# A hybrid attention and state-space layer: rotary turning of all queries, then of all keys, in place of block by block

## The chip, the cores and the metric

The kernel runs on one core of a Trainium2 chip. The metric is the device time of one execution in microseconds (us); lower is better. Every quoted window, such as 392 to 440, is in us from the start of the profiled span.

## The reference

The layer works on 2048 tokens of width 1024, in float32. The normalised input is projected once; the columns of the product are the queries, keys and values of a differential attention (4 heads, two softmax maps each, head size 64, values of 128) and the input of a diagonal state space model (S5). Both results go through one output projection, and a SwiGLU feed-forward layer and a last norm follow. Cut to what matters here:

```
hn = rms_norm(h, norm1_g)
q, k, v, u = split(hn @ w_in, [512, 1024, 1536])
q = partial_rope(q, cos, sin)      # the first 16 of 64 columns are rotated
k = partial_rope(k, cos, sin)
attn = diff_attention(q, k, v, lam)
ssm  = s5_mixer(u, ...)            # ends in y * sigmoid(y @ w_glu + b_glu)
h = h + concat(norm(attn), ssm) @ w_out
h = h + (silu(hn2 @ w_gate) * (hn2 @ w_up)) @ w_down
```

The rotation multiplies a column by a cosine and adds its partner, eight columns away, times a signed sine. The tables of cosines and sines depend on the token alone, so queries and keys share them.

## The kernel before, in words

**Matmuls.** Every product is made of three matmuls: an operand is split into a rounded high part (an ACT cast) and a rest (a DVE or POOL subtraction), and high times high, high times low and low times high are summed in PSUM (`mm3`, L516; `split`, L505). The tokens are cut into NB = 4 blocks of 512.

**Phase 1** (`phase1`, from L629) computes, in the order of the program text: the norm, the projections for the state space model, its preparation, its 16 pairs of groups (`ssm_pair`, L1020), the projections of those 16-column pieces of the queries and keys that are not rotated (L756), the values of two heads (`values(0, mm)`, L784), the rotated pieces ("q", 0) and ("k", 0) (L786 to L813), and the values of the other two heads (`values(1, mm[2:4])`, L815). Phase 2 (`phase2`, L1110) computes the gated unit after the state space model (`glu`, L1440; "the GLU" from here on), the output projections, the attention and the feed-forward layer.

**Who sets the order.** The program text doesn't. Each statement is recorded as a task with an estimated cost, its memory dependencies and a priority (`Rec`, L297; `Sched`, L176). A planner runs through the tasks and emits at each step the one that can start first; among those within 0.05 us of each other it takes the one with the lowest priority number. The engines then execute their own instructions in the order emitted. Rotations and their stores have -75, weight loads with their splits -95, projections -40, the units of the attention 0 and up, and the GLU 1000 and up. An edit in one place can thus reorder work on all engines afterwards.

**One rotation** (L803 to L813) is: 24 matmuls into one of four PSUM banks (`proj`, L669); an ACT copy of the bank into a tile `r`; a permutation matmul of `r` into the PSUM bank `tp2[0]`; on DVE that bank times the sine into `r2`; `r` times the cosine, and the sum of both, on DVE or POOL; the split (cast and subtraction) into a staging tile `z`; the store of `z` to memory, one DMA for a query (`qD`, 512 KB), two for a key (`kD`, 256 KB each: the high part, then the rest). `r` has two tiles (`turned`), `z` has two (`ups`, taken in turn, which the values after it take in turn as well), `r2` and `tp2[0]` are single.

**The tables.** `table(b)` loads the cosine and the sine of a block, two DMAs of 256 KB from `rD`, into one of two pairs of tiles. Tables 0 and 1 are loaded ahead of the loop and tables 2 and 3 in it, when the block two before has been turned. There are eight such DMAs in all.

**The weights.** Split weights lie in three slots (`ws`, L634), taken in turn by the 16 calls of `wload`. The last five calls are ("v", 1), ("q", 0), ("k", 0), ("v", 2), ("v", 3), and ("v", 3) gets the slot of ("q", 0). Raw weights pass through one single tile, the area RAW (`raws`, L635); the split of ("v", 3) is the last that reads it.

**What takes over the memory.** Areas that phase 1 has finished with become buffers of phase 2 (`room`, L1449 in `glu`). Of the three load buffers `yr` of the GLU, one is the area RAW (L1463), one lies in SD with the rotation's tables and `r2` (L1461), one in UP with the staging tiles (L1464). In a `yr` buffer come first the two halves of `w_glu` (L1473), which are cast on ACT (L1479) and subtracted on POOL or DVE (L1480), then the results of the state space model (`yD`, L1486; cast L1493, subtraction L1496). The GLU's matmuls come in groups of 24 into one PSUM tile, `fx`.

Of the kernel before, what the change touches and what calls it, by code (L numbers as in the profile page):

```python
# [14 lines left out]
AF = mybir.ActivationFunctionType  # L15
ALU = mybir.AluOpType
# [9 lines left out]
NB = S // 512  # L26
# [473 lines left out]
class K:  # L500
# [128 lines left out]
    def phase1(self):  # L629
        nc, tc, A, S = self.nc, self.tc, self.A, self.S  # L630
        rec = self.rec = self.nc = Rec(S, nc)
        misc = [a.tile for a in self.misc]
        p = Carve(misc[WS])
        ws = [p.tile([128, 2, 1024], F32R) for _ in range(3)]  # L634
        raws = [misc[RAW]]  # L635
        p = Carve(misc[UP])
        ups = [p.tile([128, 1024], F32R) for _ in range(2)]
        p = Carve(misc[SA], misc[SC])
# [9 lines left out]
        p = Carve(misc[SB])  # L648
# [5 lines left out]
        def turn(kind, tiles):  # L654
            count[kind] += 1
            return tiles[(count[kind] - 1) % len(tiles)]
# [12 lines left out]
        def proj(key, b, banks=mm):  # L669
            w = W[key].rearrange("p z (k c) -> p z k c", k=KD)  # L670
            t = turn("mm", banks)
            for k in range(KD):
                self.mm3(t, w[:, 0, k], w[:, 1, k], hn[b][0][k], hn[b][1][k], k == 0, k == KD - 1)
            return t
# [26 lines left out]
        c = Carve(*(a.tile for a in self.hnb[3]))  # L701
# [35 lines left out]
        p, c = Carve(misc[SA]), Carve(misc[SD])  # L737
# [3 lines left out]
        tables = [c.tile([128, 512]) for _ in range(2)]  # L741
# [10 lines left out]
        def store(key, b, z):  # L752
            (self.qst if key[0] == "q" else self.kst)[b][key[1]] = self.store_qk(key, b, z)

        rec.pri, rec.fair = -40.0, False
        for key in [("q", 1), ("q", 2), ("q", 3), ("k", 1), ("k", 2), ("k", 3)]:  # L756
            wload(key)
            for b in range(NB):
                t = proj(key, b)
                z = turn("up", ups).rearrange("p (c t) -> p c t", c=4)  # L760
# [27 lines left out]
        rot = [self.s2.tile([128, 512], F32, name="rot", tag=n) for n in ("tr", "t1", "t2", "pq")]  # L788
        tables, turned, r2 = [rot[0:2], tables], rot[2:4], self.gy

        def table(b):
            for j in range(2):
                rec.sync.dma_start(out=tables[b % 2][j],
                                   in_=self.rD[j][:, 512 * b:512 * b + 512][None].to_broadcast([8, 16, 512]))

        table(0)
        table(1)
        for b in range(NB):
            cos, sin = tables[b % 2]
            if b in (1, 2):  # L800
                table(b + 1)
            for key, r in zip((("q", 0), ("k", 0)), turned):
                t = proj(key, b)  # L803
                with rec.urgent(-75.0):
                    rec.scalar.activation(out=r, in_=t, func=AF.Copy, scale=0.125 if key[0] == "q" else 1.0)
                    t2 = self.tp2[0]
                    rec.tensor.matmul(t2, lhsT=self.cst["perm"], rhs=r, start=True, stop=True)
                    rec.vector.tensor_tensor(out=r2, in0=t2, in1=sin, op=ALU.mult)
                    rec.any.tensor_tensor(out=r, in0=r, in1=cos, op=ALU.mult)
                    rec.any.tensor_tensor(out=r, in0=r, in1=r2, op=ALU.add)  # L810
                    z = turn("up", ups).rearrange("p (c t) -> p c t", c=4)
                    self.split_qk(key, z, r)
                    store(key, b, z)  # L813

        values(1, mm[2:4])  # L815
        self.hn_end = [S.join(*rec.users(*(a.tile for a in self.hnb[b]))) for b in range(NB)]
# [1377 lines left out]
```

## Time and profile before

| | us |
|---|---|
| median of three executions | 2430.85 |
| lowest and highest | 2430.6, 2438.7 |
| the profiled execution's own time | 2428.99 |
| its span in the trace | 2426.9 |
| granted TensorE clock, mean over the span | 0.985 |

The profiled execution lies 1.86 us below the median, and 2.09 us of it lie outside the span. VectorE (DVE) is busy for 67% of the span, ScalarE (ACT) and GpSimd (POOL) for 43% each. In the views, PE is TensorE's matmuls, PEld its weight loads, SPq the queue from which SyncE issues nearly all DMAs. A bracket at the end of a row gives how long the engine was idle before it and what ended that. L364 is the helper through which all of phase 1 is emitted, so there the tiles tell what a row is: `pair<-hn,misc` is a projection, `pair<-misc,hn` the values, `tp<-misc,cst` the permutation matmul, and L518 to L520 with `fx` are GLU matmuls.

### The profile page before, as it was taken

The numbers are of one execution on the slowest core, as the hardware profiler recorded it, in microseconds if no ns is written. First come the engines' busy times: TensorE is split into PE (matmuls) and PEld (weight loads), VectorE is DVE, ScalarE is ACT, GpSimd is POOL, SyncE is SP. The second block draws the span as 40 slices with busy tenths as digits, with TensorE's granted clock in tenths as the row PEclk, the third lists the DMA queues.
The fourth block names the chain that finished last, engine by engine and source line by source line (L and its number), as shares of the span: only waits on it lengthen the run. The fifth ranks groups of instructions, "written<-read, shape, count | busy, mean of one in ns | idle before, by whom it ended". The sixth has DMA issues, their size and how long they took to land.

```text
span 2426.9 us, 34139 instructions
## 1 busy us (share of the span) xinstructions
PE 2335.0 (96%) x11832; PEld 1958.1 (81%) x11832; DVE 1616.7 (67%) x2577; ACT 1048.9 (43%) x2103; POOL 1041.0 (43%) x1048
## 2 busy tenths in 40 slices
PE   7999999989999999998999999999999999999998
PEld 6887797878888888876788888788888878878876
DVE  7885775247887778647877455754544576585698
ACT  7222333247877776545332333533333342242343
POOL 4134675355666556546544322222232223232244
PEclk9999999999999999998999999999999999999999
DMA  6467675665566557787886232532223255575664
GB/s 216 132 191 215 225 220 170 208 215 156 191 199 193 191 187 245 232 294 234 270 285 223 74 97 81 187 109 78 87 72 96 84 165 198 171 256 165 201 201 162
DMA packets 312174, 435.34 MB, mean 179 GB/s; under 512 B 42241, under 2 KB 187713, under 8 KB 312001
## 3 DMA queue, kind: packets, MB, share of 16 engines
q1 hardware_dynamic: 309408, 428.71, 55.4%
q10 hardware_dynamic: 2592, 4.45, 0.5%
q8 instruction: 93, 1.52, 0.3%
q14 instruction: 81, 0.66, 0.1%
HBM read 287.66 MB, written 145.42 MB: 178 GB/s over the span
## 4 chain that ended last, share of the span: by engine, by line
PE 70%; DMA 6%; DVE 4%; issue 3%; POOL 2%; ACT 2%; SPq 0%; POOLq 0%; DVEq 0%; ACTq 0%
PE pair L519 9%; PE pair L520 9%; PE pair L518 9%; PE tp L519 4%; PE tp L520 4%; PE tp L518 4%; PE fx L518 4%; PE fx L519 3%; PE fx L520 3%; PE pv L518 3%; PE pv L519 3%; PE pv L520 3%; PE pair L364 3%; DMA hn<-qD 2%; PE tp L1320 2%
## 5 line engine op out<-in xcount | busy, mean ns | idle before, releaser
L1782 ACT CAST misc<-hn 128x512 fp32r<-128x512 f32 (+1 forms) x340 | 204.8, 609 | 484.2 <-POOL hn L1902 163.0
L519 PE MATMUL pair<-hn,misc 128*128 128x512 f32 x925 | 363.4, 393 | 10.0 <-DVE hn L1783 9.9
L518 PE MATMUL pair<-hn,misc 128*128 128x512 f32 x925 | 362.2, 392 | 0.5 <-ACT misc L1782 0.4
L520 PE MATMUL pair<-hn,misc 128*128 128x512 f32 x925 | 361.9, 391 | 0.2 <-DVE misc L1783 0.2
L1783 DVE TENSOR_TENSOR misc<-hn,misc 128x512 fp32r<-128x512 f32 (+1 forms) x340 | 247.8, 732 | 113.7 <-ACT misc L1782 113.3
L364 PE MATMUL pair<-hn,misc 128*128 128x512 f32 x1152 | 282.8, 399 | 0.0
L364 PEld LDWEIGHTS pair<-hn,misc 128*128 128x128 f32 x1152 | 215.3, 191 | 45.7 <-issue 2.4
L1902 POOL TENSOR_TENSOR hn<-misc,hn 128x512 f32<-128x512 f32 (+1 forms) x68 | 99.9, 1469 | 296.5 <-DVE misc L1783 296.0
L519 PEld LDWEIGHTS pair<-hn,misc 128*128 128x128 f32 x925 | 174.6, 189 | 51.1 <-DVE hn L1783 15.6
L1909 POOL TENSOR_TENSOR hn<-hn 128x512 f32<-128x512 f32 (+1 forms) x68 | 97.1, 1428 | 256.7 <-DVE misc L1783 240.3
L518 PEld LDWEIGHTS pair<-hn,misc 128*128 128x128 f32 x925 | 174.4, 189 | 38.5 <-ACT misc L1782 0.8
L520 PEld LDWEIGHTS pair<-hn,misc 128*128 128x128 f32 x925 | 174.8, 189 | 36.5 <-DVE misc L1783 0.6
L1899 POOL TENSOR_TENSOR misc<-hn 128x512 f32<-128x512 f32 (+1 forms) x68 | 92.9, 1366 | 245.8 <-DVE misc L1783 200.1
L1221 DVE TENSOR_REDUCE small<-pair 128x1 f32<-128x1024 f32 (+7 forms) x160 | 158.2, 992 | 57.3 <-PE pair L1203 27.0
L1237 ACT ACTIVATE hn<-pair,small 128x1024 f32<-128x1024 f32 (+4 forms) x192 | 166.2, 868 | 60.1 <-DVE small L1221 27.1
L519 PE MATMUL tp<-hn,misc 128*128 128x512 f32 x454 | 177.6, 391 | 3.9 <-DVE hn L1783 3.9
L518 PE MATMUL tp<-hn,misc 128*128 128x512 f32 x454 | 177.4, 391 | 2.1 <-ACT misc L1782 1.9
L520 PE MATMUL tp<-hn,misc 128*128 128x512 f32 x454 | 177.2, 390 | 0.0
L364 POOL TENSOR_TENSOR misc<-misc,misc 128x512 f32<-128x512 f32 (+1 forms) x71 | 84.4, 1190 | 162.8 <-DVE misc L364 130.2
L1946 DVE TENSOR_TENSOR misc<-pair,misc 128x512 f32<-128x512 f32 x110 | 75.9, 690 | 95.9 <-PE pair L520 95.6
L364 POOL TENSOR_TENSOR misc<-misc 128x256 f32<-128x256 f32 (+1 forms) x128 | 102.2, 809 | 44.3 <-DVE misc L364 20.0
L364 DVE TENSOR_TENSOR misc<-misc,misc 128x512 f32<-128x512 f32 (+7 forms) x111 | 93.9, 864 | 36.5 <-ACT misc L364 30.5
(268 smaller groups left out, 5724.5 us busy)
## 6 DMA issues: line engine op xcount, KB each, us to landing
hn<-vD SPq DMA_DIRECT2D x48, 512.0 KB
hn<-kD SPq DMA_DIRECT2D x96, 256.0 KB
hn<-in_w_gate SPq DMA_DIRECT2D x44, 512.0 KB
hn<-in_w_up SPq DMA_DIRECT2D x44, 512.0 KB
fD<-misc SPq DMA_DIRECT2D x88, 256.0 KB
misc<-in_w_down SPq DMA_DIRECT2D x77, 256.0 KB
hn<-qD SPq DMA_DIRECT2D x128, 128.0 KB
hD<-misc SPq DMA_DIRECT2D x32, 512.0 KB
```

The source lines that it names most:

```text
L364: getattr(ENGINE[t.at](self.real), f)(*map(now, args), **{n: now(x) for n, x in kw.items()})
L518: nc.tensor.matmul(out, lhsT=ah, rhs=bh, start=start, stop=False, **k)
L519: nc.tensor.matmul(out, lhsT=ah, rhs=bl, start=False, stop=False, **k)
L520: nc.tensor.matmul(out, lhsT=al, rhs=bh, start=False, stop=stop, **k)
L1221: v.tensor_reduce(out=nl[:, i:i + 1], in_=x.got[sc][:, 0:w], axis=AX.X, op=ALU.max, negate=True)
L1237: a_.activation(out=z.got[rings[i]][:, 0:w], in_=x.got[sc][:, 512 * i:512 * i + w], func=AF.Exp, bias=st(n, n + 1), accum_out=acc)
L1782: hf = lambda t: a_.copy(out=dst(t)[0], in_=src())
L1783: lf = lambda t: (g_ if t.at == "pool" else v).tensor_sub(out=dst(t)[1], in0=src(), in1=dst(t)[0].bitcast(F32))
L1899: s1 = any_(n, lambda t, e: e.tensor_tensor(out=t.got[s1r][:, 0:n], in0=q(1, 0), in1=q(1, 1), op=ALU.add), *r, take=[s1r], pri=pri())
L1902: s2 = any_(n, lambda t, e: e.tensor_sub(out=q(0, 0), in0=s1.got[s1r][:, 0:n], in1=q(0, 0)), s1, s3, a11, pri=pri())
L1909: s4 = any_(n, lambda t, e: e.tensor_sub(out=q(0, 1), in0=q(0, 1), in1=q(0, 0)), s2, a12, pri=pri())
L1946: return S("dve", 1.042e-3 * w + 0.07, lambda t: v.tensor_tensor(out=(t if to is None else to).got[tm], in0=x.got[bank], in1=y.got[tm], op ...
```

## The change

The loop over blocks with queries and keys inside becomes one loop over eight rotations, first the four blocks of the queries, then the four of the keys. Both weights are still loaded ahead of the loop, and the work of one rotation is unchanged. The tile `r` still alternates. The pair of table tiles now alternates with every rotation and not with every block, and each rotation has a load of its own: table(i + 1) is recorded at rotation i (for i from 1 to 6) and may overwrite the tiles of rotation i - 1. Sixteen table DMAs take the place of eight.

```diff
-        def table(b):
+        def table(i):
+            b = i % NB
             for j in range(2):
-                rec.sync.dma_start(out=tables[b % 2][j],
+                rec.sync.dma_start(out=tables[i % 2][j],
                                    in_=self.rD[j][:, 512 * b:512 * b + 512][None].to_broadcast([8, 16, 512]))
 
         table(0)
         table(1)
-        for b in range(NB):
-            cos, sin = tables[b % 2]
-            if b in (1, 2):
-                table(b + 1)
-            for key, r in zip((("q", 0), ("k", 0)), turned):
-                t = proj(key, b)
-                with rec.urgent(-75.0):
...
+        for i in range(2 * NB):
+            key, b, r = (("q", "k")[i // NB], 0), i % NB, turned[i % 2]
+            cos, sin = tables[i % 2]
+            if 0 < i < 2 * NB - 1:
+                table(i + 1)
+            t = proj(key, b)
+            with rec.urgent(-75.0):
...
```

The left-out lines are those of one rotation, the same before and after but for their indentation.

More of the change, by code (lines that the diff above doesn't have):

```diff
@@ L797, in phase1 @@
         table(1)
-        for b in range(NB):
-            cos, sin = tables[b % 2]
-            if b in (1, 2):
-                table(b + 1)
-            for key, r in zip((("q", 0), ("k", 0)), turned):
-                t = proj(key, b)
-                with rec.urgent(-75.0):
[L805 to L813, printed above, removed]
+        for i in range(2 * NB):
[5 more added lines that the diff above has]
+            with rec.urgent(-75.0):
+                rec.scalar.activation(out=r, in_=t, func=AF.Copy, scale=0.125 if key[0] == "q" else 1.0)
+                t2 = self.tp2[0]
+                rec.tensor.matmul(t2, lhsT=self.cst["perm"], rhs=r, start=True, stop=True)
+                rec.vector.tensor_tensor(out=r2, in0=t2, in1=sin, op=ALU.mult)
+                rec.any.tensor_tensor(out=r, in0=r, in1=cos, op=ALU.mult)
+                rec.any.tensor_tensor(out=r, in0=r, in1=r2, op=ALU.add)
+                z = turn("up", ups).rearrange("p (c t) -> p c t", c=4)
+                self.split_qk(key, z, r)
+                store(key, b, z)
         values(1, mm[2:4])
```

## The prediction, made before the change was run

> **What bounds the kernel now.** I read first the page's busy times, then the granted clock and busy share by window, then the time lines of the engines around the rotations, and last the chain of waits.
>
> ```profile
> span 2426.9 us, 34139 instructions
> PE 2335.0 (96%) x11832; PEld 1958.1 (81%) x11832; DVE 1616.7 (67%) x2577; ACT 1048.9 (43%) x2103; POOL 1041.0 (43%) x1048
> ```
>
> TensorE is busy for 2335.0 of 2426.9 us. The change removes no matmul, so it can win only from the 91.9 us in which PE is idle, and from a lowered clock. The windows say where that is:
>
> ```profile
> core 0: us, PE busy (x) PEld busy (x) DVE busy (x) ACT busy (x) POOL busy (x), PEclk, DMA share, GB/s
> 392.00:440.00 48.00, 47.98 (x230) 37.58 (x229) 18.84 (x27) 14.21 (x26) 25.95 (x19) 1.00 0.45 143
> 444.00:446.00 2.00, 2.00 (x11) 2.00 (x11) 0.00 (x0) 1.05 (x2) 0.35 (x1) 0.50 0.90 239
> 454.00:456.00 2.00, 2.00 (x11) 2.00 (x11) 0.00 (x0) 0.00 (x0) 0.00 (x0) 0.50 0.93 316
> 440.00:460.00 20.00, 14.86 (x98) 14.66 (x99) 2.48 (x5) 4.53 (x10) 8.02 (x7) 0.83 0.89 264
> ```
>
> From 392 to 440, where the eight rotations lie, PE is never idle (47.98 of 48): nothing is to be won there, whatever the order. In the next 20 us it is idle for 5.14, and the clock falls to 0.50 in two windows. The time line of PE shows both stalls:
>
> ```profile
> 443.36 7.32 PE L364 MATMUL pair<-misc,hn 128*128 128x256 f32 x48 [3.38 <-DVE misc L364]
> 452.46 7.52 PE L364 MATMUL pair<-misc,hn 128*128 128x256 f32 x48 [1.77 <-DVE misc L364]
> 459.81 0.28 PE L518 MATMUL fx<-misc,misc 128*128 128x256 f32 x1
> 462.69 6.01 PE L364 MATMUL pair<-misc,hn 128*128 128x256 f32 x48
> ```
>
> These are the values after the rotations. Tiles 0 and 1 run inside the rotations' last us; tiles 2 and 3 start after 3.38 us of idling, tiles 4 and 5 after 1.77. The same 48 matmuls take 7.32 and 7.52 us behind the stalls and 6.01 later on, so the lowered clock costs 1.31 and 1.51. Together the stretch loses 3.38 + 1.77 + 1.31 + 1.51 = 7.97 us. After the first four value tiles comes one GLU group of 24 matmuls, from 459.81 to 462.69, 2.88 us.
>
> By the Trainium skill (TensorE: Matmul & The Clock Gate, Part 1) TensorE falls to half clock only after an idle window of about 3.4 us. The trace agrees for the stall of 3.38 and not for that of 1.77, behind which 454 to 456 still shows 0.50. By the rule a stall of 3.0 us, which my sum keeps below, would cost no clock and the gain would be 1.3 us more; the measurement decides.
>
> **Why PE stalls there.** The time line of ACT:
>
> ```profile
> 430.29 1.05 ACT L364 CAST misc<-misc 128x1024 fp32r<-128x1024 f32 x1 [2.48 <-PE pair L364]
> 439.21 1.14 ACT L1479 CAST misc<-misc 128x512 fp32r<-128x512 f32 x2 [2.00 <-DMA misc<-in_w_glu]
> 442.48 0.37 ACT L364 CAST misc<-pair 128x256 fp32r<-128x256 f32 x1 [1.61 <-DMA qD<-misc]
> 444.95 1.14 ACT L1479 CAST misc<-misc 128x512 fp32r<-128x512 f32 x2 [2.10 <-DMA misc<-in_w_glu]
> 450.54 1.14 ACT L1493 CAST misc<-misc 128x512 fp32r<-128x512 f32 x2 [3.50 <-DMA misc<-yD]
> 451.58 0.75 ACT L364 CAST misc<-pair 128x256 fp32r<-128x256 f32 x2
> ```
>
> On POOL, and then on SP's queue:
>
> ```profile
> 439.91 2.93 POOL L1480 TENSOR_TENSOR misc<-misc,misc 128x512 fp32r<-128x512 f32 x2
> 451.23 2.50 POOL L1496 TENSOR_TENSOR misc<-misc,misc 128x512 fp32r<-128x512 f32 x2 [3.05 <-ACT misc L1493]
> ```
>
> ```profile
> 433.38 0.40 SPq L1473 DMA_DIRECT2D misc<-in_w_glu  x1
> 438.83 0.36 SPq L364 DMA_DIRECT2D qD<-misc  x1
> 439.98 0.35 SPq L1473 DMA_DIRECT2D misc<-in_w_glu  x1
> 442.87 0.37 SPq L1486 DMA_DIRECT2D misc<-yD  x1
> ```
>
> First stall: the values from tile 2 on need a PSUM bank, which the split of tile 0 frees. That split needs the staging tile of rotation 7 (the query of block 3), whose store was issued at 438.83 and had landed when the cast began at 442.48: 3.65 us. Second stall: the cast of the next value tiles (451.58) stands on ACT behind a GLU cast (L1493) that waited 3.50 us for a load from yD, issued only at 442.87.
>
> **The change part by part.** *Nothing is removed from PE.* There are eight projections, eight permutations and eight splits, as before.
>
> *The weight slot, and what hangs on it.* ("v", 3) takes the slot of ("q", 0), and its split reads the area RAW last. Before, q's last projection is the seventh of eight, hence the cast of v3 only at 430.29 and the first load of w_glu, into RAW, at 433.38. After, it is the fourth. When is that over?
>
> ```profile
> line engine op names shapes xcount | busy us, mean ns | idle before us <-releasers
> L364 PE MATMUL pair<-hn,misc 128*128 128x512 f32 x96 | 25.1, 414 | 0.0
> ```
>
> This answer covers 404 to 432.5: 96 projection matmuls, four projections of 24. So the first four end at about 404, and v3 can be cast there, 26 us earlier, with RAW free some 2.5 us later (1.05 for the cast, the subtraction alongside), at about 406.5. From there the GLU's start can move, with the durations of before: first w_glu load 433.38 to 439.21, 5.8; from its cast to the end of the subtraction 442.84 - 439.21 = 3.6; second load 439.98 to 444.95, 5.0, and 3.6 again; load from yD 442.87 to 450.54, 7.7; to the end of its subtraction 453.73 - 450.54 = 3.2. If one buffer must serve all three, these add up to 28.9 us, and the first GLU group is ready at 406.5 + 28.9 = 435.4, against 453.7 before. PE is full until 440.0; the group (2.88 us) then lies in the first stall. And the L1493 cast no longer stands before the values' cast, so the second stall ends too. What it costs: six ACT casts and six subtractions move in among the rotations, where ACT is busy for 14.21 of 48 us and POOL for 25.95. That cover holds unless ACT waits there for a load as it did before; bounds 0 to 3.50 us, the longest such wait; I take 0, as ACT is idle for 70% of that window.
>
> *The tables.* Eight DMAs are added, 2.1 MB, and the time left for each shrinks: table(i + 1) waits for the multiplications of rotation i - 1 and is needed one rotation later, where before two rotations lay between.
>
> ```profile
> 407.62 1.28 POOL L364 TENSOR_TENSOR misc<-misc 128x512 f32<-128x512 f32 x1 [8.69 <-DMA misc<-rD]
> 413.95 1.30 POOL L364 TENSOR_TENSOR misc<-misc 128x512 f32<-128x512 f32 x1 [1.26 <-PE tp L364]
> 436.96 2.99 POOL L364 TENSOR_TENSOR misc<-misc,misc 128x512 f32<-128x512 f32 x2 [0.41 <-PE tp L364]
> ```
>
> ```profile
> 415.27 1.27 SPq L364 DMA_DIRECT2D misc<-rD  x2
> ```
>
> ```profile
> L364 SPq DMA_DIRECT2D misc<-rD x3: 575/584/605, 399.5 to 401.7; - x3
> ```
>
> The multiplication of rotation 2 starts at 413.95 and takes 1.30; SP issued the next table at 415.27, 0.02 later, its second DMA some 0.69 after the first (two in 1.27). A table DMA issued at 401.7 was awaited until 407.62, so T = 5.9 us from issue to use. Rotations 4, 6 and 8 then follow 0.71 + T after the end of 2, 4 and 6: rotation 8 multiplies at 415.25 + 3 x (0.71 + T) + 2 x 1.30 = 419.98 + 3T, at T = 5.9 at 437.7, against 436.96 before: 0.7 us late. Other landings bound T:
>
> ```profile
> 426.04 7.22 DMA kD<-misc
> 434.07 5.27 DMA kD<-misc
> 512.86 10.00 DMA hn<-qD
> ```
>
> At 5.27 there is no delay, at 7.22 it is 4.7, at 10.0, the landing of an attention load in the same trace, 13.0. I take 0.7, since the first row is a table load itself. While a table load waits on SP for a multiplication, the rotations' stores and the GLU's loads stand behind it; the issues themselves take 8 x 0.6 = 5 us of a queue that has room.
>
> By the Trainium skill (DMA: Bandwidth & Descriptors, Anatomy of one DMA) a DMA has a fixed cost of about 2.0 us plus its bytes at 436 GB/s, fitted on the other, GpSimd path; my estimate from that is 2.6 us for a table, the 0.7 would be 0, and the forecast would stay. The trace's 5.9 disagrees, under load.
>
> *The store behind the first value tile.* Rotation 7 is now a key, whose last DMA landed after 5.27 to 7.22 us and not 3.65: 1.6 to 3.6 us more. I take 1.6, the later row, nearest to the place.
>
> **The sum.** Values tiles 2 and 3 may start at 443.36 + 0.7 + 1.6 = 445.7. PE is idle from 440.0, 5.7 us, of which one GLU group fills 2.9; 2.8 to 3.0 remain, so half clock as before, 7.32 us, to 453.0. Tiles 4 and 5 follow without a stall at 6.01, to 459.0. By then the same work is done that ended at 462.69: 3.7 us gained. A second group (its fx bank must be read by ACT first) would fill the rest and save the 1.3 of clock as well: 445.7 + 12.0 = 457.7 against 462.69 + 2.88, 7.9 gained, the same as the 7.97 lost now. I take one group, -3.7, which against the profiled execution gives 2428.99 - 3.7 = 2425.3; against the median, 1.86 higher, 2427.2 us.
>
> Later work gets the 3.7 us if PE has no slack there. The rest of phase 2 has some:
>
> ```profile
> 440.00:1100.00 660.00, 625.74 (x3991) 546.65 (x3992) 443.59 (x695) 421.76 (x949) 362.99 (x442) 0.97 0.68 213
> ```
>
> ```profile
> PE pair L1199 <- DMA hn<-qD: 7.3, 6, 2.8
> ```
>
> Up to 1100 it is idle for 34.3 us, 29.1 beyond the two stalls, 7.3 of them waits for query loads (the second row is from the waits of PE over the span). The planner will order this stretch anew, with a result no row shows. I take 0, with bounds of -7.3 (all these loads relieved, as 1.5 MB of GLU loads leave the busy 440 to 460) and a like amount above.
>
> **The rivals.**
>
> *No fill.* The planner leaves the GLU, its last priority, behind the rotations, and both stalls stay, 0.7 late with the rotations: 2431.6. For it: ACT, POOL and SP serve rotations first. Against it: they have idle time from 404 on. Chance 0.20.
>
> *The tables become the bound (slower).* 16 table loads share the DMA engines with the stores and now the GLU's loads; if T is 10.0, rotation 8 is 13.0 late, the staging store adds 1.6, the second stall (1.8) is hidden, nothing fills: +12.8, 2443.7. It decides from 3T - 16.98 - 0.2 = 12.2, T = 9.8. For it: 10.00 exists in the trace. Against it: it belongs to a stretch with a DMA share of 0.6 to 0.9, and 392 to 440 shows 0.45. Chance 0.12.
>
> *All at once (faster).* Two groups fill the stall, -7.9, and the query loads no longer hold PE, -7.3: 2430.85 - 15.2 = 2415.7. Against it: the loads' waits lie from 510 on, far from the relief. Chance 0.13.
>
> *The attention is planned anew* for better or worse by more than the rotations matter, from +13 to -13. Chance 0.13, spread evenly over faster, same and slower. That the order wouldn't change at all is excluded: banks, `r` and staging tiles are taken in recorded order.
>
> **How the numbers follow.** The forecast, 2427.2, has 0.42. The range goes down to two groups and half of the query loads, 2430.85 - 7.9 - 3.6 = 2419.4, and up to the late tables, 2444; outside are the all-at-once case and the far ends of the replanning, about 0.2. About what a measurement of this kernel can tell from no change is 0.5%, 12.2 us: under 2418.7 or over 2443.0. Faster: 0.13 + 0.04 = 0.17. Slower: 0.04 and three quarters of the tables' case, 0.13. The same: 0.70.
>
> **What would show it.** Right: the 128x1024 cast before 410, w_glu loads (L1473) at about 407, an L518 group before 445, one stall and not two between 440 and 460, and POOL's last rotation within 1 us of 436.96. Wrong: GLU loads still after 430 (no fill), POOL or DVE waiting for rD in several rotations (tables), or PE waits from 392 to 440, of which there are none now. I am wrong as a whole if the time is over 2444 or under 2419.

## The result, and the profile after

The change made the kernel slower. The median after is 2447.14 us (six executions, 2441.11 to 2448.02), of the kernel before beside it 2432.24 us (six, 2428.56 to 2438.70): ratio 1.0058, 95 % interval 1.0043 to 1.0072, which is 14.1 us. The prediction was 2427.2 us with a range up to 2444.0, so its sign was wrong and its range 3.1 us too low. The profiled execution after took 2446.91 us.

The head of the page after:

```profile
span 2445.1 us, 34183 instructions
PE 2338.1 (96%) x11832; PEld 1959.9 (80%) x11832; DVE 1611.8 (66%) x2582; ACT 1046.0 (43%) x2097; POOL 1034.3 (42%) x1049
```

PE is busy for 3.1 us more than before (2335.0), in a span that is 18.2 us longer: what was added is mostly time in which PE stands idle. The busy time by window, after:

```profile
core 0: us, PE busy (x) PEld busy (x) DVE busy (x) ACT busy (x) POOL busy (x), PEclk, DMA share, GB/s
415.00:425.00 10.00, 9.72 (x39) 7.04 (x38) 5.11 (x6) 4.00 (x7) 7.99 (x6) 1.00 0.80 240
425.00:435.00 10.00, 7.49 (x29) 5.10 (x28) 3.82 (x5) 3.05 (x6) 6.00 (x5) 1.00 0.70 241
430.00:440.00 10.00, 6.27 (x27) 4.81 (x26) 4.20 (x5) 3.57 (x6) 6.30 (x6) 0.88 0.63 208
436.00:446.00 10.00, 9.78 (x59) 8.83 (x60) 3.64 (x5) 3.14 (x6) 4.84 (x4) 0.83 0.57 197
392.00:440.00 48.00, 43.99 (x193) 33.60 (x192) 21.13 (x28) 14.46 (x26) 23.85 (x18) 0.97 0.58 177
440.00:460.00 20.00, 17.27 (x123) 16.59 (x123) 5.13 (x8) 5.28 (x12) 6.71 (x5) 0.89 0.53 187
460.00:700.00 240.00, 220.37 (x1513) 198.29 (x1513) 139.76 (x230) 140.74 (x335) 117.88 (x152) 0.95 0.63 194
700.00:1100.00 400.00, 379.47 (x2312) 323.24 (x2311) 285.29 (x453) 263.61 (x578) 231.65 (x281) 0.98 0.68 213
```

And before, in windows that were not shown yet (in 400 to 406 the first table loads were under way):

```profile
400.00:406.00 6.00, 6.00 (x32) 4.55 (x31) 0.69 (x1) 1.79 (x4) 0.00 (x0) 1.00 0.50 150
415.00:425.00 10.00, 10.00 (x40) 7.16 (x39) 3.95 (x6) 3.06 (x5) 8.21 (x7) 1.00 0.64 212
425.00:435.00 10.00, 10.00 (x49) 7.83 (x48) 4.83 (x6) 3.98 (x6) 6.20 (x5) 1.00 0.56 170
460.00:700.00 240.00, 223.26 (x1564) 201.64 (x1564) 152.63 (x241) 154.71 (x364) 127.98 (x157) 0.96 0.60 190
700.00:1100.00 400.00, 387.62 (x2333) 330.34 (x2332) 288.47 (x450) 262.52 (x575) 226.98 (x278) 0.99 0.71 224
```

Two things are to be seen. In 392 to 440, where PE had no gap, it now loses 4.0 us. In 440 to 460 it gains 2.4 (17.27 against 14.86): the hoped-for filling of the stall is there. But by far the most PE time is lost later, among the attention's units: 2.9 us in 460 to 700 and 8.2 in 700 to 1100. These two differences are to be read with care, for kernels as fast as before differ from it there too: e7 and e8, which come below, have 219.11 and 220.13 us in 460 to 700, which is no more than after, and 386.42 and 386.24 in 700 to 1100. Against these the loss in 460 to 700 is gone, and that in 700 to 1100 is 6.8 to 7.0 us.

POOL, and DVE once, show why the rotations fell behind:

```profile
421.48 1.70 DVE L364 TENSOR_TENSOR misc<-misc,misc 128x512 f32<-128x512 f32 x1 [1.86 <-DMA misc<-rD]
429.13 1.27 POOL L364 TENSOR_TENSOR misc<-misc 128x512 f32<-128x512 f32 x1 [3.60 <-DMA misc<-rD]
439.88 1.27 POOL L364 TENSOR_TENSOR misc<-misc 128x512 f32<-128x512 f32 x1 [3.29 <-DMA misc<-rD]
446.10 2.65 POOL L364 TENSOR_TENSOR misc<-misc,misc 128x512 f32<-128x512 f32 x2 [1.88 <-DMA misc<-rD]
```

The fourth rotation waits for its table on DVE; the fifth, the seventh and the eighth wait on POOL. SP's queue has the issues of the last pair, and of the loads and stores around:

```profile
410.75 0.41 SPq L1474 DMA_DIRECT2D misc<-in_w_glu  x1
...
424.84 2.46 SPq L364 DMA_DIRECT2D qD<-misc  x2
428.21 2.80 SPq L364 DMA_DIRECT2D misc<-rD  x2
...
435.32 0.59 SPq L364 DMA_DIRECT2D misc<-rD  x1
435.97 0.60 SPq L364 DMA_DIRECT2D kD<-misc  x1
436.66 0.58 SPq L364 DMA_DIRECT2D misc<-rD  x1
```

From the last table's second DMA (436.66) to its use (446.10) are 9.4 us; from that of the pair before (the row at 428.21 covers two issues in 2.80, so the second began near 430.4) to 439.88 are 9.5. The last rotation comes at 446.10 against 436.96, 9.1 later, and the attention's first load (`hn<-vD`) at 461.33 against 450.60, 10.7 later. In 415 to 425 and in 425 to 435 the DMA engines are busy for 0.80 and 0.70 of the time, before for 0.64 and 0.56; while the last two pairs were under way, 430 to 440 and 436 to 446, it was 0.63 and 0.57.

The time lines of ACT and of PE, after:

```profile
406.59 1.05 ACT L364 CAST misc<-misc 128x1024 fp32r<-128x1024 f32 x1 [0.45 <-PE pair L364]
430.04 1.14 ACT L1480 CAST misc<-misc 128x512 fp32r<-128x512 f32 x2 [2.50 <-DMA misc<-in_w_glu]
433.98 0.62 ACT L364 CAST misc<-misc 128x512 fp32r<-128x512 f32 x1 [2.81 <-DMA qD<-misc]
```

```profile
436.22 1.12 PE L364 MATMUL tp<-misc,cst 128*128 128x512 f32 x2 [3.73 <-ACT misc L364]
445.26 0.28 PE L518 MATMUL fx<-misc,misc 128*128 128x256 f32 x1
451.03 0.48 PE L518 MATMUL fx<-misc,misc 128*128 128x256 f32 x1 [2.73 <-ACT misc L1517]
498.85 7.50 PE L364 MATMUL pair<-misc,hn 128*128 128x256 f32 x48 [2.37 <-DVE misc L364]
1003.85 0.76 PE L1200 MATMUL pair<-hn 128*128 128x512 f32 x1 [6.04 <-DMA mixD<-hn]
1090.79 1.12 PE L1692 MATMUL tp<-cst,misc 128*128 128x128 f32 x4 [3.68 <-ACT misc L1695]
```

The cast of ("v", 3) is 24 us earlier, as foreseen, and the first GLU group runs at 445.26. A second new cost stands beside the tables: the fifth rotation's split waits until 433.98 for its staging tile. There are two of these, used in turn, so it is the tile of the third query, whose store was issued at 424.84 (the first of the two in that row): 9.1 us, where the query's store that ACT waited for in the kernel before took 3.65. PE's new stall of 3.73 us follows from that. The last two rows are stalls that the kernel before does not have in this size; its longest between 460 and 1100 is 2.83 us.

### The profile page after: what moved, and what is told of

It is laid out like the page before. It is cut to its first block, busy times and chain, and to the rows that moved or that the text cites. A ratio compares the mean times of both kernels' runs of the same rounds, so it can differ in the third digit from the quotient of the medians.

```text
span 2445.1 us, 34183 instructions
## 1 busy us (share of the span) xinstructions
PE 2338.1 (96%) x11832; PEld 1959.9 (80%) x11832; DVE 1611.8 (66%) x2582; ACT 1046.0 (43%) x2097; POOL 1034.3 (42%) x1049
## 4 chain that ended last, share of the span: by engine, by line
PE 50%; DVE 3%; issue 1%; ACT 0%; POOL 0%; DMA 0%; POOLq 0%; DVEq 0%; ACTq 0%
PE pair L519 9%; PE pair L520 9%; PE pair L518 8%; PE tp L519 4%; PE tp L520 4%; PE tp L518 4%; PE fx L520 2%; PE fx L518 2%; PE fx L519 2%; PE pv L520 2%; PE pv L519 2%; PE pv L518 2%; DVE hn L1784 1%; DVE misc L1784 1%; PE tp L1692 0%
## 5 line engine op out<-in xcount | busy, mean ns | idle before, releaser
L519 PEld LDWEIGHTS pair<-hn,misc 128*128 128x128 f32 x931 | 176.3, 189 | 47.1 <-DVE hn L1784 10.7
```

Source lines behind the costliest of these rows:

```text
L519: nc.tensor.matmul(out, lhsT=ah, rhs=bl, start=False, stop=False, **k)
```

## The experiments

Two theories stood at the start. *Tables*: the new loads come late, push the rotations back and with them all that follows. *Arrangement*: any edit here makes the planner order phase 2 anew, and the new order is worse, whatever the rotations do. Later a third was added, that the order of the rotations costs something by itself. In all results the ratio is to the kernel before, run beside the experiment, with its 95 % interval.

| kernel | median us | ratio | interval |
|---|---|---|---|
| after | 2447.14 | 1.0058 | 1.0043 to 1.0072 |
| e1_four_tables | 2447.03 | 1.0067 | 1.0041 to 1.0092 |
| e2_before_16_loads | 2437.36 | 1.0028 | 1.0015 to 1.0042 |
| e3_after_order2_before | 2440.45 | 1.0043 | 1.0025 to 1.0060 |
| e4_glu_late | 2450.02 | 1.0079 | 1.0049 to 1.0108 |
| e5_after_short | 2442.14 | 1.0035 | 1.0022 to 1.0047 |
| e6_short_order2_before | 2440.09 | 1.0033 | 1.0021 to 1.0044 |
| e7_before_short16 | 2431.68 | 0.9996 | 0.9985 to 1.0006 |
| e8_before_replanned | 2431.88 | 0.9999 | 0.9990 to 1.0008 |
| e9_keys_first_short | 2444.30 | 1.0044 | 1.0028 to 1.0060 |
| e10_short_3_staging | 2446.36 | 1.0046 | 1.0030 to 1.0062 |
| e11_before_3_staging | 2436.93 | 1.0010 | 0.9999 to 1.0021 |
| e12_pairs_of_blocks | 2456.18 | 1.0093 | 1.0075 to 1.0110 |
| e13_before_replanned_1015 | 2453.57 | 1.0091 | 1.0076 to 1.0106 |
| e14_before_replanned_1022 | 2451.41 | 1.0076 | 1.0061 to 1.0092 |
| e15_after_replanned_1018 | 2453.30 | 1.0088 | 1.0072 to 1.0103 |
| e16_short_replanned_1018 | 2447.66 | 1.0065 | 1.0051 to 1.0079 |

**All four tables resident.** The queries come first, and four pairs of table tiles are loaded once, into memory that the state space pairs have left.

```diff
-        def table(i):
-            b = i % NB
+        a, b = self.s1.tags["sT"], [self.s1.tags[x] for x in ("xh", "xl")]
+        tables += [[a[:, 0:512], a[:, 512:1024]], b]
+        def table(b):
...
-            if 0 < i < 2 * NB - 1:
-                table(i + 1)
...
-        table(0)
-        table(1)
+        for b in range(NB):
+            table(b)
```

> The changed order (all queries, then all keys), but the tables of all four blocks stay in memory: eight table loads as before the change, none of which waits for a rotation; two table pairs lie in memory that the state space model has finished with, so the GLU gets one load buffer for its split results only after the rotations. Theory A (late tables: the changed kernel's last rotation multiplies at 446 instead of 437, and with it all memory that the attention waits for comes free 10 us late): the last rotation is back at 437 to 440, the first key and query loads of the attention before 454, and the time is 2429 to 2436. Theory B (the planner's new order of phase 2 costs the time, whatever the rotations do): 2441 to 2450 though the rotations end by 440. Theory C (the GLU's early loads and casts crowd the rotations): the last rotation is still at 443 or later, 2438 to 2447.

Ratio 1.0067, as slow as after, but the run does not clear the tables. POOL's first rotation:

```profile
415.00 1.28 POOL L364 TENSOR_TENSOR misc<-misc 128x512 f32<-128x512 f32 x1 [12.77 <-DMA misc<-rD]
```

Seven of the loads were issued together, and the first rotation waited for them until 415.00, 11.1 us after the first of them was issued (403.89). Before, with three loads, these were 8.2 us (399.45 to 407.62). In this execution everything was already 4.4 us behind when the loads were issued. The wait had only moved to the first rotation, and the last one was at 447.42, no earlier than in after. So this run could not tell the theories apart. It shows one thing besides: with these loads and little else under way, the mean busy share of the DMA engines is no more than 0.53.

```profile
409.00:411.00 2.00, 2.00 (x14) 1.62 (x11) 0.00 (x0) 1.29 (x3) 0.00 (x0) 1.00 0.53 205
```

**Sixteen loads in the order of before.** Only the tables are changed, to a load of its own for every rotation.

```diff
-            if b in (1, 2):
-                table(b + 1)
-            for key, r in zip((("q", 0), ("k", 0)), turned):
+            for n, (key, r) in enumerate(zip((("q", 0), ("k", 0)), turned)):
+                i = 2 * b + n
+                cos, sin = tables[i % 2]
+                if 0 < i < 2 * NB - 1:
+                    table(i + 1)
```

> The order before the change, with the changed kernel's way of loading tables: each rotation has a load of its own into the pair of the rotation before the last, sixteen DMAs. The planner's order of everything else is that of before. Theory A: rotations wait for their tables by 2 to 4 us several times, the last one multiplies at 442 to 447, and the time is 8 to 15 us above before. Theory B: the order of phase 2 is that of before, so within 3 us of before. Theory C: without the GLU's early loads a table takes the 5.9 us of before, the last rotation is less than 2 us late, within 4 us of before.

Ratio 1.0028: 6.8 us, with the planner's order of all other work as in before. POOL again:

```profile
428.24 1.28 POOL L364 TENSOR_TENSOR misc<-misc 128x512 f32<-128x512 f32 x1 [2.78 <-DMA misc<-rD]
444.17 2.75 POOL L364 TENSOR_TENSOR misc<-misc,misc 128x512 f32<-128x512 f32 x2 [1.13 <-DMA misc<-rD]
```

The last rotation is at 444.17, 7.2 late, and the attention's first load at 457.54, 6.9 late (1.4 of it was there at the first rotation, 409.03 against 407.62); the loss at the end is about the same. The added whole loads, with all that they hold up, thus cost about half of what the change costs, without any new order of keys and queries.

**The order of phase 2 forced back.** The planner's choices in phase 2 are replaced by the list of those that it made for before (which task, on which engine); phase 1 is that of after.

```diff
-                c = [(s, t) for s, t in ((self.start(t, e), t) for t in l) if s is not None
-                     and (len(t.engs) == 1 or self.choose(t) == e)]
+                c = [(s, t) for s, t in ((self.start(t, e), t) for t in l if self.may(t, e)) if s is not None
+                     and (len(t.engs) == 1 or t.no is not None or self.choose(t) == e)]
...
+    def may(self, t, e):
+        return t.no is None or self.want[self.at] == (t.no, e)
```

> The changed kernel's phase 1 with the tasks of phase 2 (GLU, output projections, attention, feed-forward) emitted in exactly the order, and on the engines, that they have in the kernel before. Theory A: rotations late by 9 us as in the changed kernel, and the time 9 to 15 us above before (2441 to 2447). Theory B: within 4 us of before (2428 to 2436) although the rotations are as late as in the changed kernel. Theory C: as theory A if the GLU's first loads still come before 415, as theory B if they come after 430.

Ratio 1.0043, lower than after, but the intervals overlap. Inconclusive by itself: a forced order was made for other times of the same work.

**The gated unit held back.** The area RAW is given to the GLU only when the fourth query has been stored.

```diff
-        room(RAW, yr)
+        c_raw = S.join(rooms[RAW], self.qst[3][0])
+        S.join(c_raw, fn=lambda t: yr.free.append((t.end, Carve(self.misc[RAW].anew()).tile(*kinds[yr]))))
```

> The changed kernel, but the area RAW is handed to the GLU only once the fourth query has been stored, so that the GLU's first weight load is issued near 433, as before the change, and not near 411. Theory A: the tables are still late, the last rotation multiplies at 443 to 447, time 2440 to 2448. Theory B: no forecast better than 2432 to 2448, as this is one more order of phase 2. Theory C: a table takes about 6 us, the last rotation is back at 437 to 439, and the time within 4 us of before.

Ratio 1.0079. The first load of `w_glu` is issued at 433.56 in place of 410.75, and the time gets no better, though the last rotation comes at 439.81 in place of 446.10. The loads did share in the tables' lateness: where the first GLU load was issued only behind the last table, that table took about 7.5 us (here) and 7.9 (e2), against 9.4 in after. But this kernel too has a new order of phase 2, and its interval overlaps that of after, so it does not settle what the GLU's early loads cost in all. It shows that the lateness of the rotations is not the whole of the loss.

**Short loads.** From the third rotation on a table load moves 64 of 512 columns; the planner is told the old size, so that its order is that of after, instruction for instruction. The rotations from there on use old table columns.

```diff
+                n = 64 if i > 1 else 512
-                rec.sync.dma_start(out=tables[i % 2][j],
-                                   in_=self.rD[j][:, 512 * b:512 * b + 512][None].to_broadcast([8, 16, 512]))
+                rec.sync.dma_start(out=tables[i % 2][j][:, 0:n],
+                                   in_=self.rD[j][:, 512 * b:512 * b + n][None].to_broadcast([8, 16, n]))
```

> The changed kernel with the same order of all instructions, but from the third rotation on a table load moves 64 of the 512 columns (the other columns of the tables stay stale, so those rotations compute with wrong tables): the same waits, shorter transfers. Theory A (late tables hold the rotations, these the memory that the attention's first loads wait for, and this is carried to the end one for one): no rotation after the second waits for rD, the last one multiplies at 436 to 439 and not at 446, the attention's first loads come at 451 to 453 and not at 461, and the time is 8 to 10 us below the changed kernel, 2437 to 2440. Theory B (what costs is the planner's new order of phase 2, and the lateness is absorbed): the loads come earlier but the time stays within 4 us of the changed kernel.

> As the run before this one (queries first, short table loads, stale tables), but phase 2 emitted in the order of the kernel before. Both suspected costs are taken away. Theory A and B together: attention loads at 450 to 453 and a time of 2429 to 2435, as before the change; left over is at most the store behind the first value tile, about 1.6 us. If queries first costs something else, such as the GLU's early load or the two stores of a key, the time is above 2437 here too.

> A control for the short loads: the order before the change, a table load for every rotation, short from the third on (stale tables). If short loads only take the lateness away, this is within 3 us of the kernel before and 4 to 8 below the one with sixteen whole loads; if moving 1.8 MB less relieves the DMA queues by itself, it is faster than before by 3 us or more.

The second adds the forced order of phase 2, the third is the control: the sixteen loads in the order of before, short as well. The control is at 0.9996, so short loads take the whole cost of e2 away (1.0028). After with short loads is at 1.0035. No rotation behind the first waits for a table there, but two expectations were missed: the last rotation is at 441.72, not 436 to 439 (2.5 us of its 4.8 of delay lie ahead of the first rotation), and the attention's first load at 456.12, not 451 to 453. PE and the rest of the stretch in e5:

```profile
392.00:440.00 48.00, 46.19 (x213) 35.84 (x211) 21.98 (x32) 15.87 (x29) 28.87 (x19) 1.00 0.50 153
440.00:460.00 20.00, 19.07 (x156) 18.64 (x155) 6.33 (x11) 5.61 (x13) 7.45 (x7) 1.00 0.65 196
460.00:700.00 240.00, 217.40 (x1526) 194.53 (x1525) 146.26 (x236) 146.02 (x346) 118.73 (x153) 0.98 0.62 194
700.00:1100.00 400.00, 381.50 (x2302) 324.14 (x2301) 282.70 (x447) 260.24 (x573) 230.13 (x280) 0.99 0.69 216
```

With tables on time, PE is busy for 65.26 us in 392 to 460, 2.4 more than in before (62.84) and with 369 matmuls where before had 328. So here the queries-first order does what the prediction wanted of it. And yet the kernel is slower by 0.35 %: against before, PE's busy time is 5.9 us less in 460 to 700 and 6.1 less in 700 to 1100; against e7 and e8, whose rows follow in this order, it is 1.7 to 2.7 and 4.7 to 4.9.

```profile
460.00:700.00 240.00, 219.11 (x1536) 198.42 (x1535) 152.73 (x240) 152.94 (x361) 127.80 (x156) 0.96 0.60 190
700.00:1100.00 400.00, 386.42 (x2326) 328.85 (x2325) 286.12 (x447) 261.40 (x574) 227.34 (x278) 0.99 0.70 222
460.00:700.00 240.00, 220.13 (x1537) 198.87 (x1538) 153.72 (x241) 154.70 (x364) 128.92 (x157) 0.96 0.61 189
700.00:1100.00 400.00, 386.24 (x2326) 331.32 (x2326) 283.78 (x449) 261.84 (x572) 220.74 (x274) 0.99 0.70 221
```

The forced order does not mend this: 1.0033, where 2429 to 2435 us had been expected with both suspected costs taken away and 2440.09 were measured. So neither theory, nor both together, accounts for the rest.

**A new arrangement alone.** The kernel before, with the planner's cost factor for the matmuls of phase 2 at another value. Tables, rotations and stores are untouched.

```diff
-            t.engs = {engs: cost * 1.02}
+            t.engs = {engs: cost * (1.02 if self.no is None else JIT)}
```

> The kernel before, where only the planner's estimate of a matmul's cost in phase 2 is changed, from 1.02 to 1.018 of the nominal; the instructions are the same ones, phase 1 and the rotations are in the same order, and phase 2 is in the same order until about 466 us. Theory A: the order of phase 2 is worth little, within 4 us of before. Theory B: a new order of phase 2 is a draw, and before is a good one: 4 to 15 us above before, with PE idle in other places between 470 and 1100.

JIT = 1.018: ratio 0.9999. The new order is a small one: PE leaves the old order of instructions only at 595 us. Arrangement seemed to cost nothing, and I turned to the order of the rotations itself.

**The order of the rotations.** Keys first and then queries, with short loads; a third staging tile, with and without queries first; and the order q0 q1 k0 k1 q2 q3 k2 k3 with eight whole loads, in which each table serves two rotations.

```diff
-            key, b, r = (("q", "k")[i // NB], 0), i % NB, turned[i % 2]
+            key, b, r = (("k", "q")[i // NB], 0), i % NB, turned[i % 2]
```

```diff
+        ups3 = [*ups, view(self.s1.tags["sT"], [128, 1024], F32R)]
...
-                z = turn("up", ups).rearrange("p (c t) -> p c t", c=4)
+                z = turn("up3", ups3).rearrange("p (c t) -> p c t", c=4)
```

```diff
-            key, b, r = (("q", "k")[i // NB], 0), i % NB, turned[i % 2]
-            cos, sin = tables[i % 2]
-            if 0 < i < 2 * NB - 1:
-                table(i + 1)
+            key, b, r = (("q", "k")[i // 2 % 2], 0), 2 * (i // 4) + i % 2, turned[i % 2]
+            cos, sin = tables[i % 2]
+            if i in (3, 4):
+                table(i - 1)
```

> All keys first, then all queries (the key weight also loaded first, so the last value weight is still free after the fourth rotation); table loads as in e5 move 64 of 512 columns from the third rotation on, so those rotations use old table columns. Theory A, the keys' stores: the last four rotations are then queries, whose store is one DMA and lands in about 3.7 us in place of two in 5.3 to 7.2, so the staging tiles come free for the values earlier and the first attention loads (hn<-vD) are issued by about 452 (456.12 in e5); ratio to before 1.000 to 1.001. Theory B, all rotations of one kind in a row cost it, whichever comes first (the first attention unit needs both): as e5, 1.003 to 1.004.

> e5 (queries first, short table loads from the third rotation, so old table columns) with a third staging tile for the rotations and the values after them, in memory that the state space pairs have left. Theory A (the keys' stores hold the two staging tiles): the waits of ACT for vD and kD stores between 440 and 470 (up to 6.8 us) go, first attention loads by 452, ratio to before 1.000 to 1.001, or under 1 if the values gain too. Theory B: attention loads may move, the time stays at 1.003 to 1.004.

> The kernel before with the same third staging tile, nothing else changed: the control for e10. If the staging tile as such helps, it does so here as well: the stalls of 3.38 and 1.77 us with their lowered clock go, at most 8 us, ratio 0.997 to 1.000. If the planner's new order behind it costs more than that, over 1.000; then a gain of e10 counts against this one.

> Whole table loads, eight as before, in the order q0 q1 k0 k1 q2 q3 k2 k3: each table pair serves two rotations. Theory A: the last two rotations are keys, so of the 8 us about half remain; tables 2 and 3 have one rotation (6.3 us) to land in, at 6 us they are on time; ratio 1.001 to 1.003. Theory B (rotations of one kind in a row, four long, are the cost): 1.000, a version as good as before. If late tables alone counted: at 9 us of landing two waits of 3 us, one behind the other, last rotation at 440 to 443.

Keys first, 1.0044: it is no faster with the queries' stores at the end, though this is a new arrangement too. The third staging tile brings the attention's first load to 449.6 with queries first (456.12 without) and to 447.5 with the order of before; the times are 1.0046 and 1.0010. With queries first, an attention that starts 6.5 us earlier gave nothing back, in an arrangement that is again another. The pairs were meant as a better version and are the slowest of all, 1.0093. ACT, and then PE, in that kernel:

```profile
433.98 1.14 ACT L1480 CAST misc<-misc 128x512 fp32r<-128x512 f32 x2 [6.06 <-DMA misc<-in_w_glu]
438.25 0.60 ACT L364 ACTIVATE misc<-pair 128x512 f32<-128x512 f32 x1 [2.37 <-DVE misc L364]
```

```profile
438.90 2.07 PE L364 MATMUL tp<-misc,cst 128*128 128x512 f32 x2 [4.99 <-ACT misc L364]
```

A GLU cast stands in ACT's queue ahead of a rotation and waits 6.06 us for its load; behind it the rotation's split and copy are late, and PE idles for 4.99.

**More arrangements.** e13 and e14 are e8 with JIT at 1.015 and 1.022; e15 and e16 are after, and after with short loads, with JIT at 1.018.

> The kernel before with the planner's cost factor for phase 2's matmuls at 1.015 in place of 1.02: the rotations, tables and stores as before, the order from about the first attention loads on anew. Theory A (the order of the rotations costs 8 us by itself): ratio 0.999 to 1.001, as e8. Theory B (a new arrangement costs, and by chance): 1.002 or more, here or in e14, with the added idle time of PE spread over the first attention units.

> As e13 with the factor 1.022; the order differs from some attention units later on. Theory A: 0.999 to 1.001. Theory B: 1.002 or more, here or in e13.

> The kernel after (whole table loads, queries first) with the factor 1.018. Theory A: 1.005 to 1.007, as after. Theory B: the time moves with the arrangement, 1.002 to 1.010; under 1.004 would show that part of after's loss lay in its arrangement.

> e5 (queries first, short table loads from the third rotation, old table columns) with the factor 1.018. Theory A: 1.003 to 1.004, as e5. Theory B: it moves by 0.2 % or more from e5; at 1.001 or less no loss would be left for the order of the rotations.

The kernel before, with nothing but the order of phase 2 changed, is slower by 22.1 us (1.0091) and 18.5 us (1.0076): more than the change itself. The windows of e13:

```profile
392.00:440.00 48.00, 48.00 (x230) 37.63 (x230) 18.95 (x28) 14.35 (x26) 25.52 (x19) 1.00 0.44 143
440.00:460.00 20.00, 15.30 (x112) 14.82 (x112) 2.74 (x5) 4.31 (x10) 8.06 (x7) 0.91 0.88 261
460.00:700.00 240.00, 218.94 (x1531) 196.77 (x1530) 148.44 (x237) 150.83 (x359) 124.87 (x155) 0.96 0.59 183
700.00:1100.00 400.00, 381.04 (x2281) 322.26 (x2280) 282.57 (x446) 258.39 (x567) 221.49 (x273) 0.99 0.69 216
```

The rotations are those of before (48.00 of 48), the stretch behind them is no worse (15.30 against 14.86), and its first attention load is issued at 450.69 (450.60). The loss begins after 460: 4.3 us to 700 and 6.6 from there to 1100 (against e7 and e8 0.2 to 1.2 and 5.2 to 5.4). Up to 1100 this looks like after and like e5. Behind 1100 it does not: PE idles there for 41.6 us in e13, 35.6 in after and 33.8 in before. So e13 shows how much an order alone can cost, and not that the loss of after is the same one. PE's time line shows two stalls close in time to those of after, the first at another instruction, which waits for ACT and not for a DMA, the second at the same transposition (L1692 there):

```profile
991.69 0.58 PE L524 MATMUL pv<-hn,hn 128*128 128x256 f32 x1 [4.30 <-ACT hn L1333]
1089.34 0.93 PE L1698 MATMUL tp<-cst,misc 128*128 128x128 f32 x4 [4.18 <-ACT misc L1701]
```

The same factor of 1.018 that left before as it was made after slower by 0.30 points (1.0058 to 1.0088) and after with short loads by 0.30 (1.0035 to 1.0065); the intervals of the first pair touch, those of the second are apart. And in both arrangements the short loads are worth 0.23 points, 5.6 us.

## Why the prediction was wrong, point by point

*The weight slot and the fill: right in mechanism.* v3 was cast at 406.59 (about 404 to 406.5 had been said), the first load of `w_glu` was issued at 410.75, the first group ran at 445.26, some 10 us later than worked out, and PE's idle time in 440 to 460 fell from 5.14 to 2.73 us. Where the tables were on time (e5), PE did 41 matmuls more up to 460. But the step from there to the end, "Tiles 4 and 5 follow without a stall ... 3.7 us gained", gave nothing: no run turned work done earlier into a shorter time.

*The cover at 0: held here, by luck.* ACT waited for GLU loads among the rotations, 2.50 us before 430.04, inside the bounds; PE's stall came from a store. In e12 the same kind of wait was 6.06 us, above the bound of 3.50, and cost PE 4.99. That ACT is idle for 70 % of a window says nothing about a cast that waits in its queue ahead of a rotation.

*The tables: the first term that failed.* "T = 5.9" and "0.7 late" became T = 9.4 to 9.5 and 9.1. The formula 419.98 + 3T gives 448.2 at 9.4, close to 446.10, but in part by luck: it has the fourth, the sixth and the eighth rotation wait, and those that waited were the fourth, the fifth, the seventh and the eighth, the fourth for about 6.7 us from its table's issue and the fifth for 8.8. Its input was off by 3.5 us. The row was a table load, but while it was under way nothing else was except other table loads: the DMA share was 0.50 (400 to 406, before). Where the new loads run, beside stores and GLU loads, it is 0.80 at first (415 to 425, after). The loads raised it themselves: with short ones (e5) that window is at 0.54. The GLU's loads, which the same change moved there, add some 1.5 to 1.9 of the 3.5 us; that is a rough estimate from the 7.9 of e2 and the 7.5 of e4, where the first GLU load was issued only behind the last table. But the mean share does not tell how long a load takes: the two pairs that took 9.5 and 9.4 ran at 0.63 and 0.57. Nor does a share of 0.50 mean that half of the room is free for another table: seven table loads at once (e1) bring it to 0.53 and no higher. In the trace a table load signals its landing in eight parts and a query's store in sixteen, so a table seems to use half of the DMA engines. No run spread one over all of them, so what that would save is not shown. I argued against the rival with the mean of 0.45 over 392 to 440 *of before*, and left out that the change itself adds to it. The cost of the whole loads, 5.6 to 7.8 us, is shown: by e2 against e7, whose intervals lie apart, and with the same sign and size by after against e5 and e15 against e16, whose intervals overlap at their ends. By the Trainium skill (DMA: Bandwidth & Descriptors, Anatomy of one DMA) my estimate was 2.6 us for such a load; 9.4 disagrees by a factor above three. The prediction said that the forecast would stay by that estimate; with the 0.7 at 0 it would have been 0.7 us lower.

*The store: the size that was taken, the reason not shown.* From the last rotation to the first attention load are 13.6 us before and 15.2 after, 1.6 more; that the key's store made this difference no run shows. The store that did stop PE was that of the third query, at 9.1 us in place of 3.65, and it stopped it among the rotations, where the prediction had no cost.

*The later order: the second term that failed.* "I take 0, with bounds of -7.3 ... and a like amount above", and a chance of 0.13 for an attention planned anew. e13 and e14 show that a new order of phase 2 alone, with the order of all instructions up to 460 as before, takes +22.1 and +18.5 us, and e8 that it can take 0. The bound was far too narrow: an order can cost more than the late tables do. I had read from before that PE has 29.1 us of slack in its waits and thought of it as something to gain; it shows as well how much waiting this stretch has to give out if the order fits less.

*The rivals.* "The tables become the bound" came true in part: its price was 12.8, the total 14.1, but the tables are only 5.6 to 7.8 of that, and would not have passed 0.5 % alone. The rest, 6.3 to 8.5 us, lies downstream of the rotations; the largest part of it that the windows of e5 show is 4.7 to 4.9 us in 700 to 1100. A new order is large enough to make it (e13, e14), but that it did was not shown, and before's own order, forced on the kernel with short loads, left 1.0033.

*What stays open.* What makes the rest of the loss, with tables on time. Whether turning all queries first costs anything of itself. The five kernels with four rotations of one kind in a row and short loads lie between 1.0033 and 1.0065; five with before's rotations and tables, or those with a third staging tile, lie at 1.0000 (before itself), 0.9999, 1.0010, 1.0076 and 1.0091. The two sets overlap, so no cost of the order is needed, and none is excluded. Against a pure matter of arrangement speaks that before's own order of phase 2, forced on queries first, gave 1.0033; that it fits worse there because it was made for loads that come 6 us earlier is argued, not shown. Which property of before's and e8's orders makes them good was not found.

## What to carry to other kernels

Price an added transfer by a row that lies where the transfer will run and under the load that the change itself will bring there, not by a row of its own kind beside which nothing else was under way. Where a planner orders the work, an edit upstream draws a new order downstream; make a control that changes only the order (a cost factor, a tie broken otherwise) and try several values, as one may move nothing and the next 20 us, before a gain or a loss of that size is put down to the edit. Work pulled forward into a stall is a gain only if the stretch that it is taken from can do without it.

## What the runs showed of the hardware that was not expected

A 256 KB table load took 5.9 us from issue to use with only other table loads under way (DMA share 0.50), and 9.4 to 9.5 beside stores and GLU loads, though the share then was only 0.57 to 0.63; seven of them held the first rotation for 11.1 us from the first issue (three before: 8.2), at a share of no more than 0.53. The store of a query went from 3.65 to 9.1 us.

TensorE's clock fell after shorter stalls than thought. After the stall of 2.37 us ahead of 498.85 the 48 matmuls took 7.50 us (6.01 at full clock), and the window behind it, after, reads:

```profile
500.00:502.00 2.00, 2.00 (x11) 2.00 (x11) 0.00 (x0) 0.00 (x0) 0.00 (x0) 0.50 1.07 372
```

In e5, after 1.87 us, the clock stayed at 1.00 (494 to 496), and the 48 matmuls took 6.02 us:

```profile
493.49 6.02 PE L364 MATMUL pair<-misc,hn 128*128 128x256 f32 x48 [1.87 <-DVE misc L364]
```

The Trainium skill (TensorE: Matmul & The Clock Gate, Part 1) puts the fall behind an idle window of about 3.4 us; the stall of 2.37 us disagrees, and the 1.77 us of the kernel before, which came 9 us behind a longer stall, disagrees too.
